# Expert weights with neighbouring rows in one partition, in a two-layer diffusion backbone on one core

## The chip, the cores and the metric

The kernel runs on 1 core of one Trainium2 chip, in float32. The metric is the device time of one execution in microseconds (us), as the median of several runs.

## The reference, cut to what matters

Two layers work on 256 latent tokens of width 1024 (and on 256 context tokens in the first layer's mixer). A layer has a mixer (latent attention with an RG-LRU in layer 0, a Hyena convolution in layer 1) and then a mixture of 16 experts, of which each token takes 2. Both halves are modulated by vectors `sh`, `sc`, `g` that come from a conditioning vector `c` and the big matrix `ada_w`.

```
mod = silu(c) @ ada_w[layer] + ada_b[layer]          # 6 vectors of 1024: sh1, sc1, g1, sh2, sc2, g2
x = x + g1 * mixer(rms_norm(x, norm1_g) * (1 + sc1) + sh1)
h = rms_norm(x, norm2_g) * (1 + sc2) + sh2
s = sigmoid(h @ router_w) ...                        # 16 scores, best group of 4, best 2 in it
for e in range(16):
    y = y + gates[..., e:e+1] * ((silu(h @ w1[e]) * (h @ w3[e])) @ w2[e])
x = x + g2 * y
```

`w1[e]` and `w3[e]` are 1024 x 512, `w2[e]` is 512 x 1024: 2 MiB each, 6 MiB an expert, 192 MiB (201 million bytes) for both layers. Every expert's weights are loaded in full.

## The kernel before, in words

The width of 1024 is contracted 128 rows at a time, with a row of the weights in each of 128 partitions. Everything that meets a weight is therefore cut into 8 chunks (`k`), and chunk `k` holds features `128k` to `128k + 127`. `mat` gives the DMA's source: for `w1` and `w3` a tile of 1 MiB has four chunks, so a partition receives 4 rows that lie 128 rows apart, each a run of 512 floats (2 KB) in HBM; for `w2` a tile has two chunks, 2 runs of 1024 floats (4 KB). In the last pass `w2` is cut by columns and its runs are of 2 KB.

**Loads.** All big loads are planned in `order` and issued one after the other from SP by `emit` (L219). They go into rings of 1 MiB buffers: `w` (9 buffers), `sp` (8, shared with activations), `x` (`extra`, 1 in layer 0 and 3 in layer 1). A load waits at SP for the matmuls that still read its buffer. Experts 4 to 15 are sorted by load at run time, and their loads take the expert's number from a register.

**A mixture of experts** (`moe`) has 7 passes (`PASSES`), six with two experts and one with four. A pass runs `up` for `w1` (L1244), `silu`, `up` for `w3` (L1244), `times` (L1254), `turn` (four transposes, L1259, that bring the hidden activation's 512 features to partitions), `down` (L1272), `weigh` (L1278 to L1282: gates and `g2`, split into a high and a low half for TensorE) and `back` (L1289, L1291: adds to `x`). Tokens are picked by a one-hot matrix `P` in `gather` (L1204, L1215), which contracts the normalised tokens `yh` and `yl` (high and low halves, made by `high`, L627 on ACT, and `low_`, L633 on DVE) and applies the modulation (L1218, L1220). In layer 0 the passes are interleaved with the building of the Hyena filters (L1443, L1470, L1499, L1500).

**The router** stands ahead of it: `enter` (L576 to L580) transposes `x` in 16 pieces, `weights` (L589) multiplies by the router's weights, `choose` (L655 to L663) ranks, `count` (L670 to L677) counts and gives each token a place, `sort`, `gates` and `rounds` follow. Between `in_order("PAD")` in `run` and the `in_order` that ends it in `moe`, the order of TensorE, ACT and DVE is written out by hand; elsewhere a planner with a simulated clock chooses each engine's order from what is ready.

**The modulation in the background.** `bg` does steps of `ada_step`: a matrix's products are summed over `k` on DVE (L451) or TensorE (L442, then ACT L446). Some steps later the 128 partial sums are added up: by transposes and a reduction (`ada_columns`, L372, L379 to L384) for `sh` and `sc`, or by a matmul with ones (`ada_row`, after a DVE instruction L422 that adds the bias; L391, L392) for `g`. At the start of each mixture one matrix is worked through by `bg(KD)`: `sc2` of layer 1 in layer 0, `g2` of layer 1 in layer 1. `bg_all()` then finishes it.

Of the kernel before, what the change touches and what calls it, by code (L numbers as in the profile page):

```python
# [9 lines left out]
F32 = mybir.dt.float32  # L10
# [4 lines left out]
OP = mybir.AluOpType  # L15
# [11 lines left out]
PASSES = ((0, 1), (2, 3), (8, 9), (4, 5, 6, 7), (10, 11), (12, 13), (14, 15))  # L27
LAST = len(PASSES) - 1
QUAD = 4
NW = 9  # L30
N8 = 8
NX = (1, 3)
# [61 lines left out]
def _pack_params(v):  # L94
    pk = np.zeros((128, NPK), np.float32)

    def cols(name, a):
        a = np.asarray(a)
        pk[:a.shape[0], PK[name]:PK[name] + a.shape[1]] = a

    def chunks(a):
        return np.asarray(a).reshape(-1, 128).T

    cols("c", chunks(v["c"]))
    cols("cc", chunks(v["c_ctx"]))
    cols("n1", chunks(v["norm1_g"]))
    cols("n2", chunks(v["norm2_g"]))
    cols("qn", chunks(v["mla_q_norm_g"]))
    cols("kvn", chunks(v["mla_kv_norm_g"]))
    cols("cw", chunks(v["lru_conv_w"]))  # L110
    cols("cb", chunks(v["lru_conv_b"]))
    cols("ba", chunks(v["lru_b_a"]))
    cols("bx", chunks(v["lru_b_x"]))
    cols("lam", chunks(v["lru_lambda"]))
    cols("hw", chunks(v["hy_conv_w"]))
    cols("hb", chunks(v["hy_conv_b"]))
    cols("rb", np.broadcast_to(np.asarray(v["router_b"])[None, :], (128, 16)))
    cols("rw", np.asarray(v["router_w"]).reshape(8, 128, 16).transpose(1, 0, 2).reshape(128, 128))
    cols("adab", chunks(v["ada_b"]))
    cols("dec", chunks(v["hy_decay"]))  # L120
    cols("skip", chunks(v["hy_skip"]))
    cols("b1", np.asarray(v["hy_b1"]).reshape(64, 1))
    cols("f1", np.asarray(v["hy_freq1"]).reshape(64, 1))
    cols("b2", np.tile(np.asarray(v["hy_b2"]).reshape(64, 1), (2, 1)))
    cols("f2", np.tile(np.asarray(v["hy_freq2"]).reshape(64, 1), (2, 1)))
    cols("w1", np.asarray(v["hy_w1"])[0])
    cols("w2", np.asarray(v["hy_w2"])[0])
    return pk
# [38 lines left out]
def build(tc, A, dbg=None, stop=None):  # L167
# [43 lines left out]
    def emit(n):  # L211
        for _ in range(n):
            if emitted[0] < len(order):
                key, src, shape = order[emitted[0]]
                emitted[0] += 1
                i = emitted[0] - 1
                t = apart[i]() if i in apart else wp.tile([128, 2048], F32, tag="w", name=nm("w"))
                v = t[:shape[0], :shape[1] * shape[2]].rearrange("p (k f) -> p k f", k=shape[1])
                nc.sync.dma_start(v, src() if callable(src) else src)  # L219
                made[key] = v  # L220

    def get(key):
# [47 lines left out]
            if len(order) < end:  # L270
                plan(key, src, shape)

    def expert(nme, l, e, r0, nk, c0, nf):

        w = A["moe_" + nme]
        if e < STATIC:
            return mat(w[l, e], r0, nk, c0, nf)
        return lambda: mat(w[l, bass.ds(chosen[l][e - STATIC], 1)].rearrange("o k f -> (o k) f"), r0, nk, c0, nf)

    def moe_tiles(l):  # L280
        for j, es_ in enumerate(PASSES):
            for nme in ("w1", "w3"):
                for kk in range(2):
                    for e in es_:
                        yield ((nme, l, e, kk), expert(nme, l, e, kk * 512, 4, 0, 512), (128, 4, 512))
            for h in range(2):
                for e in es_:
                    if j < LAST:
                        yield (("w2", l, e, h), expert("w2", l, e, h * 256, 2, 0, 1024), (128, 2, 1024))
                    elif h == 0:  # L290
                        yield (("w2", l, e, 0), expert("w2", l, e, 0, 4, 0, 512), (128, 4, 512))
            if j == LAST:
                for h in range(2):
                    for e in es_:
                        yield (("w2", l, e, 1 + h), expert("w2", l, e, h * 256, 2, 512, 512), (128, 2, 512))

    plan_moe(0)
    for n in range(6):
# [69 lines left out]
    def ada_columns(l, s, hf, use, e, four, n):  # L368

        p2 = ps()  # L370
        for m in range(4):
            T.transpose(p2[:, m * 128:m * 128 + 128], e[:, m * 128:m * 128 + 128], ident)  # L372
        pv = p2.rearrange("p (m q r) -> p m q r", m=4, q=4)
        b = pc("adab", l * 48 + s * 8 + hf * 4, 4)
        for i in range(n):
            kind = ("c" if i else "") + ("1" if s < 3 else "2")
            o = mc(l, use + kind)[:, hf * 4:hf * 4 + 4]
            if four:
                V.tensor_reduce(o, pv[:, :, :, i], axis=mybir.AxisListType.X, op=OP.add)  # L379
            else:  # L380
                V.tensor_reduce(o, p2.rearrange("p (m r) -> p m r", m=4), axis=mybir.AxisListType.X, op=OP.add)
            V.tensor_tensor(o, o, b, op=OP.add)
            if use == "sc":
                V.scalar_tensor_tensor(o, o, 1.0, pc("n1" if s < 3 else "n2", l * 8 + hf * 4, 4),  # L384
                                       op0=OP.add, op1=OP.mult)
# [82 lines left out]
    def bg_all():  # L468
        while ada_step():
            pass  # L470
# [68 lines left out]
    def in_order(engines=""):  # L539
# [3 lines left out]
        if engines:  # L543
            manual.append(tc.manual_schedule(engines={ENG[e] for e in engines}))
            manual[0].__enter__()

    class router:


# [21 lines left out]
        def enter(self, i):  # L571

            t, n = divmod(i, 2)
            p = ps()
            for k in range(4):
                T.transpose(p[:, k * 128:k * 128 + 128], x[:, t, (4 * n + k) * 128:(4 * n + k) * 128 + 128], ident)  # L576
            S.activation(self.alloc().bitcast(BF16)[:, :512], x[:, t, n * 512:n * 512 + 512], AF.Square,
                         accum_out=self.ss[:, i:i + 1])
            self.xT[i] = self.alloc()
            S.activation(self.xT[i], p, AF.Copy)  # L580
# [42 lines left out]
        def high(self, t):  # L623

            for n in range(2):
                c = slice(n * 512, n * 512 + 512)
                S.activation(self.y[0][:, t, c], x[:, t, c], AF.Copy, scale=self.r[t])  # L627

        def low_(self, t):

            for n in range(2):
                c = slice(n * 512, n * 512 + 512)
                V.scalar_tensor_tensor(self.y[1][:, t, c], x[:, t, c], self.r[t], self.y[0][:, t, c].bitcast(F32),  # L633
                                       op0=OP.mult, op1=OP.subtract)

        def rank(self, v, n, out):

# [523 lines left out]
    def moe(l, route, ws, filler=None, fills=((0, 0, 0),) * 8, budget=0, late=None, prepare=None, finish=None):  # L1161
# [94 lines left out]
        def turn(j):  # L1256
            p = ps()
            for k in range(4):
                T.transpose(p[:, k * 128:k * 128 + 128], act[j][:, k * 128:k * 128 + 128], ident)  # L1259
            at = act[j] = w2("at")  # L1260
            for i in range(2):
                copy(i, at[:, 256 * i:256 * i + 256], p[:, 256 * i:256 * i + 256])
# [50 lines left out]

        def again(nme, e, k, n=0):
            t = wk.tile([128, 512], F32, tag="t2", name=nm("wr"), bufs=WT2[l])
            nc.sync.dma_start(t, A["moe_" + nme][l, e, k * 128:k * 128 + 128, n * 512:n * 512 + 512])
            return t

        ada_alloc[0] = lambda n, *shape: [w2(n) for _ in range(2)]
# [5 lines left out]
        gather(0, firsts, True)  # L1325
        in_order(ORDER[1 + 2 * l])
        next(steps, None)
        bg_all()
        route.gates()
        route.sort(w2("srt"))  # L1330
        _, chosen[l] = nc.values_load_multi_w_load_instructions(
# [6 lines left out]
        for j in range(LAST + 1):  # L1338
            up(j, "w1", first, firsts)
            a = silu(j)  # L1340
            if j == LAST:
                with tc.issue_after(a.ins):
                    S.activation(warm, ones[:, 0:1], AF.Sqrt)
            if j:
                back(j - 1, 0)
                back(j - 1, 1)
            else:
                slots(0, gate, firsts)
                slots(1, gate, firsts)
            fill(fills[j][0])  # L1350
            up(j, "w3", first, firsts)
            times(j)
            if j % 2 and j < LAST:
                d = j // 2 + 1
                place(d, pos, firsts)
                gather(d, firsts)
                for i in range(2 * d, min(2 * d + 2, LAST + 1)):
                    slots(i, gate_, firsts)
                fill(fills[j][1] - 1)
            else:  # L1360
                fill(fills[j][1])
            turn(j)
            fill(fills[j][2])
            down(j, 0, first, firsts)
            weigh(j, 0)
            if j == LAST:
                fill(99)
                down(j, 1, first, firsts, (0, 1))
                back(j, 0, (0,))
                back(j, 1, (0,))  # L1370
                if late:
                    late(0)
                squares(0)
                down(j, 1, first, firsts, (2, 3))
            else:
                down(j, 1, first, firsts)
            weigh(j, 1)
# [395 lines left out]
```

## Time and profile before

| | us |
|---|---|
| median of 3 runs | 947.39 (945.4 to 949.32) |
| the profiled execution's own time | 945.29 |
| its span, first to last instruction | 943.4 |
| TensorE (PE) busy | 863.5 (92%) |
| DVE busy | 462.8 (49%) |
| ACT busy | 228.9 (24%) |

The granted TensorE clock was 0.975 of full speed over the span. All DMA moved 289.33 MB in 130567 packets, 307 GB/s over the span. A matmul's end is modelled, so PE's busy time also covers starts that are further apart than they need to be. The layers' mixtures run from about 260 to 520 us and from about 697 to 932 us.

### The profile page before, as it was taken

The page shows a single profiled execution, that of the slowest core. Times are in us where ns is not written, and L with a number is a line of the kernel's source. Part 1 is how long each engine was busy: PE and PEld are TensorE (multiplying, and loading weights), DVE is VectorE, ACT ScalarE, POOL GpSimd, SP SyncE. Part 2 cuts the span into 40 slices and gives each one's busy share as a digit, 9 for nine tenths or more (in the row PEclk, how much of TensorE's full clock was granted, in tenths as well). Part 3 has the DMA queues.
Part 4 walks back from the last instruction along what each step waited for, and adds up shares of the span by engine and source line. Part 5 has one row for each costly group of instructions (what it writes and reads, how often), then busy time and mean ns, then how long its engine had stood idle before and what let it go on. Part 6 is the DMA issues. An engine that isn't in the chain of part 4 may idle for free. (4 is left out here: it accounts for less than half of the span.)

```text
span 943.4 us, 10841 instructions
## 1 busy us (share of the span) xinstructions
PE 863.5 (92%) x3976; PEld 447.2 (47%) x3976; DVE 462.8 (49%) x1124; ACT 228.9 (24%) x446; POOL 15.7 (2%) x21
## 2 busy tenths in 40 slices
PE   3998999999999999899998599999989999988984
PEld 2345655574553534333433487776553532423431
DVE  5469785771643454536433648756272323122123
ACT  3276414430411221313122222211031110100112
POOL 0000000000000010101000000000000000000000
PEclk9999999999899999999999799999979999999998
DMA  9957689476799999999999673643199999999993
GB/s 351 353 187 248 224 269 369 165 248 242 244 385 397 329 384 387 395 390 396 396 338 372 229 267 131 223 151 116 57 386 352 389 395 387 404 389 396 396 387 144
DMA packets 130567, 289.33 MB, mean 307 GB/s; under 512 B 6828, under 2 KB 8876, under 8 KB 130500
## 3 DMA queue, kind: packets, MB, share of 16 engines
q1 hardware_dynamic: 129428, 286.39, 82.9%
q10 hardware_dynamic: 1072, 2.10, 0.7%
q8 instruction: 36, 0.59, 0.3%
q14 instruction: 31, 0.25, 0.1%
HBM read 287.42 MB, written 1.05 MB: 306 GB/s over the span
## 5 line engine op out<-in xcount | busy, mean ns | idle before, releaser
L1244 PE MATMUL ps<-w,xe 128*64 128x512 f32 (+1 forms) x696 | 174.6, 597 | 2.4 <-DMA w<-in_moe_w 2.4
L1244 PEld LDWEIGHTS ps<-w,xe 128*64 128x64 f32 (+1 forms) x696 | 50.4, 129 | 87.5 <-issue 79.2
L1272 PE MATMUL ps<-w,at 128*64 128x512 f32 (+1 forms) x344 | 86.0, 597 | 4.5 <-DMA w<-in_moe_w 2.7
L1594 PE MATMUL ps<-xt,w 128*128 128x256 f32 x384 | 87.4, 388 | 1.8 <-ACT xt L1558 1.8
L1594 PEld LDWEIGHTS ps<-xt,w 128*128 128x128 f32 x384 | 74.4, 195 | 14.6 <-ACT xt L1558 2.1
L1291 DVE TENSOR_TENSOR x<-x,ps 128x512 f32<-128x512 f32 x56 | 36.9, 683 | 64.6 <-PE ps L1289 64.6
L1278 DVE SCALAR_TENSOR_TENSOR ye<-ps,gs,grow 128x512 f32<-128x512 f32 x28 | 20.9, 748 | 83.1 <-PE ps L1272 83.1
L1244 PE MATMUL ps<-sp,xe 128*64 128x512 f32 (+1 forms) x216 | 54.5, 598 | 1.4 <-DMA sp<-in_moe_w 1.2
L451 DVE SCALAR_TENSOR_TENSOR e<-w,sg,e 128x512 f32<-128x512 f32 x70 | 51.4, 744 | 3.0 <-DMA w<-in_ada_w 2.3
L1272 PEld LDWEIGHTS ps<-w,at 128*64 128x64 f32 (+1 forms) x344 | 26.7, 130 | 50.6 <-issue 40.0
L1280 ACT ACTIVATE yeh<-ye 128x512 fp32r<-128x512 f32 x28 | 17.6, 630 | 117.5 <-DVE ye L1278 117.5
L1244 PE MATMUL ps<-x,xe 128*64 128x512 f32 (+1 forms) x112 | 37.4, 595 | 1.6 <-DMA x<-in_moe_w 1.6
L1254 DVE TENSOR_TENSOR th<-th,ps 128x512 f32<-128x512 f32 x14 | 9.6, 687 | 59.0 <-PE ps L1244 59.0
L1244 PEld LDWEIGHTS ps<-sp,xe 128*64 128x64 f32 (+1 forms) x216 | 16.7, 132 | 30.0 <-issue 26.3
L1220 ACT ACTIVATE xe<-ps,modc 128x256 f32<-128x256 f32 (+1 forms) x32 | 15.8, 539 | 58.0 <-DVE xe L1218 58.0
L517 PE MATMUL ps<-w,x 128*128 128x512 f32 x64 | 28.4, 595 | 0.7 <-ACT x L1608 0.7
L1249 ACT ACTIVATE th<-ps 128x512 f32<-128x512 f32 x14 | 8.4, 597 | 84.1 <-PE ps L1244 68.5
L835 PE MATMUL ps<-hT,w 128*128 128x512 f32 x64 | 28.0, 593 | 0.4 <-DMA w<-in_ev_w_in 0.4
L517 PE MATMUL ps<-w,mix 128*128 128x512 f32 x64 | 28.2, 594 | 0.0
L1272 PE MATMUL ps<-sp,at 128*64 128x512 f32 (+1 forms) x112 | 26.0, 598 | 2.3 <-ACT at L345 1.7
L442 PE MATMUL ps<-w,cs 128*32 128x512 f32 x160 | 27.1, 714 | 0.0
L930 PE MATMUL ps<-w,hT 128*128 128x288 f32 (+1 forms) x96 | 26.8, 434 | 0.0
(355 smaller groups left out, 1311.0 us busy)
## 6 DMA issues: line engine op xcount, KB each, us to landing
w<-in_moe_w SPq DMA_DIRECT2D x126, 1024.0 KB, 13.9
w<-in_ada_w SPq DMA_DIRECT2D x48, 1024.0 KB, 7.3
sp<-in_moe_w SPq DMA_DIRECT2D x41, 1024.0 KB, 14.6
x<-in_moe_w SPq DMA_DIRECT2D x21, 1024.0 KB, 14.2
w<-in_od_w_in SPq DMA_DIRECT2D x12, 1024.0 KB, 6.8
w<-in_ev_w_in SPq DMA_DIRECT2D x4, 1024.0 KB, 10.9
w<-in_ev_w_out SPq DMA_DIRECT2D x4, 1024.0 KB, 7.9
w<-in_moe_w SPq DMA_DIRECT2D x8, 512.0 KB, 9.8
```

Of the source, the lines that this page charges most:

```text
L442: T.matmul(part[hf][32 * q:32 * q + 32, :], cs[:, k - 3 + q, :], get(("ada", l, s, hf, k // 4))[:, q, :], start=(k == 3), stop=(k == 7), t ...
L451: V.scalar_tensor_tensor(eh, w[hf], c, eh, op0=OP.mult, op1=OP.add)
L517: T.matmul(po[t][n], a[:, k, t * 128:t * 128 + 128], b[:, n * 512:n * 512 + 512], start=(k == korder[0] and i == 0), stop=(k == korder[-1] ...
L835: T.matmul(uxp[b], get(("wux", hf))[:, k % 4, b * 128:b * 128 + 128], hT[hf][:, k % 4, :], start=(k == 0), stop=(k == KD - 1))
L930: T.matmul(p[:, :n], hT[k // 4][:, k % 4, t * 128:t * 128 + 128], get((w, k // 4))[:, k % 4, :], start=(k == 0), stop=(k == KD - 1))
L1220: S.activation(e[:, k, :w], p[:, w:2 * w], AF.Identity, scale=sc[:, k:k + 1], bias=sh[:, k:k + 1])
L1244: T.matmul(p[room * i:room * i + room, :], xe[j // 2][:, k, o:o + room], weight(nme, e, k), start=(k == 0), stop=(k == KD - 1), tile_posit ...
L1272: T.matmul(p[room * i:room * i + room, :], act[j][:, o:o + room], weight("w2", e, k, n), start=(k == 0), stop=(k == 3), tile_position=(0, ...
L1278: V.scalar_tensor_tensor(e, po[j, n], gs[j], grow[l, 5][:, n * 512:n * 512 + 512], op0=OP.mult, op1=OP.mult)
L1280: S.activation(h, e, AF.Copy)
L1291: V.tensor_tensor(xs, xs, p, op=OP.add)
L1594: T.matmul(pb, w[:, k % 4, b * 128:b * 128 + 128], hT[:, k, :], start=(k == 0 and b % 2 == 0), stop=(k == KD - 1 and b % 2 == 1))
```

## The change

The contraction is cut otherwise: a partition now holds neighbouring rows. For `w1` and `w3` partition `p` of tile `a` gets rows `512a + 4p` to `512a + 4p + 3`, and for `w2` rows `256h + 2p` and `256h + 2p + 1`, which is 8 KB in one stretch of HBM and 8 KB in one stretch of the partition. Only the last pass's `w2`, cut by columns, keeps runs of 2 KB; its one tile with two blocks is issued as two DMAs. Chunk `k` then holds every fourth feature of a 512 (every second of a 256 for `w2`), and all that meets it is reordered to match: the router's transposes read `x` with a step of 4 floats, `high` and `low_` read `x` with a step of 4 and write in the new order, `turn` reads with a step of 2, the transposes of `ada_columns` read with a step of 4 for the modulation of the mixture (`s >= 3`), and `norm2_g`, `ada_b` and `router_w` are packed in the new order on the host. Apart from that, `bg_all()` stands later in `moe`: after `up` for `w1`, `silu` and `slots` of the first pass, instead of ahead of `gates` and `sort`. The kernel before already sums some matrices' modulation on TensorE; this is not part of the change.

```diff
+GROUP = {"w1": 4, "w3": 4, "w2": 2}
...
+    def by_rows(a):
+        return np.asarray(a).reshape(-1, 128, 4).transpose(1, 0, 2).reshape(128, -1)
...
-    cols("n2", chunks(v["norm2_g"]))
+    cols("n2", by_rows(v["norm2_g"]))
...
-                nc.sync.dma_start(v, src() if callable(src) else src)
+                a = src() if callable(src) else src
+                if len(a.shape) == 3:
+                    nc.sync.dma_start(v, a)
+                else:
+                    g = a.shape[2]
+                    for b in range(a.shape[1]):
+                        nc.sync.dma_start(v[:, b * g:b * g + g], a[:, b])
...
+    def expert_rows(w, nme, c0, nf):
+        return w.rearrange("(a p k) f -> p a k f", p=128, k=GROUP[nme])[:, :, :, c0:c0 + nf]
...
-            return mat(w[l, e], r0, nk, c0, nf)
+            return expert_rows(w[l, e], nme, c0, nf)[:, a0:a0 + na]
...
-            T.transpose(p2[:, m * 128:m * 128 + 128], e[:, m * 128:m * 128 + 128], ident)
+            T.transpose(p2[:, m * 128:m * 128 + 128], e[:, m * 128:m * 128 + 128] if s < 3 else e[:, m::4], ident)
...
+    def by_rows(v):
+        return v.rearrange("p (k q) -> p k q", k=4)
...
-                T.transpose(p[:, k * 128:k * 128 + 128], x[:, t, (4 * n + k) * 128:(4 * n + k) * 128 + 128], ident)
+                T.transpose(p[:, k * 128:k * 128 + 128], x[:, t, n * 512 + k:n * 512 + 512:4], ident)
...
-                S.activation(self.y[0][:, t, c], x[:, t, c], AF.Copy, scale=self.r[t])
+                S.activation(by_rows(self.y[0][:, t, c]), x[:, t, c].rearrange("p (q k) -> p k q", k=4), AF.Copy,
+                             scale=self.r[t])
...
-                V.scalar_tensor_tensor(self.y[1][:, t, c], x[:, t, c], self.r[t], self.y[0][:, t, c].bitcast(F32),
-                                       op0=OP.mult, op1=OP.subtract)
+                V.scalar_tensor_tensor(by_rows(self.y[1][:, t, c]), x[:, t, c].rearrange("p (q k) -> p k q", k=4),
+                                       self.r[t], by_rows(self.y[0][:, t, c].bitcast(F32)), op0=OP.mult, op1=OP.subtract)
...
-                T.transpose(p[:, k * 128:k * 128 + 128], act[j][:, k * 128:k * 128 + 128], ident)
+                T.transpose(p[:, k * 128:k * 128 + 128], act[j][:, k // 2 * 256 + k % 2:k // 2 * 256 + 256:2], ident)
...
         next(steps, None)
-        bg_all()
         route.gates()
...
                 slots(0, gate, firsts)
                 slots(1, gate, firsts)
+                bg_all()
```

## Rows read from the trace of the kernel before

**Rows 1.** The page, parts 2 and 5: DMA in 40 slices; the costliest matmuls (mean ns).

```profile
GB/s 351 353 187 248 224 269 369 165 248 242 244 385 397 329 384 387 395 390 396 396 338 372 229 267 131 223 151 116 57 386 352 389 395 387 404 389 396 396 387 144
...
L1244 PE MATMUL ps<-w,xe 128*64 128x512 f32 (+1 forms) x696 | 174.6, 597 | 2.4 <-DMA w<-in_moe_w 2.4
```

**Rows 2.** Windows, second mixture; the last columns are granted clock, DMA share, GB/s.

```profile
720.00:925.00 205.00, 188.40 (x914) 73.65 (x912) 52.67 (x99) 22.47 (x44) 0.00 (x0) 1.00 1.04 394
```

**Rows 3.** PE's waits on loads from 265 to 932 us: total, times, longest.

```profile
PE ps L1272 <- DMA w<-in_moe_w: 2.7, 4, 0.7
...
PE ps L1244 <- DMA w<-in_moe_w: 2.4, 2, 1.5
...
PE ps L1244 <- DMA x<-in_moe_w: 1.6, 1, 1.6
...
PE ps L1244 <- DMA sp<-in_moe_w: 1.2, 1, 1.2
...
PE ps L1272 <- DMA sp<-in_moe_w: 0.6, 1, 0.6
```

**Rows 4.** Timeline of PE: first and last of the first mixture's three such waits.

```profile
386.47 0.63 PE L1244 MATMUL ps<-w,xe 128*32 128x512 f32 x3 [1.51 <-DMA w<-in_moe_w]
...
406.96 3.62 PE L1272 MATMUL ps<-w,at 128*32 128x512 f32 x20 [0.68 <-DMA w<-in_moe_w]
```

**Rows 5.** Timeline of PE at the last such wait: start, duration of the group.

```profile
910.48 3.26 PE L1244 MATMUL ps<-sp,xe 128*64 128x512 f32 x13
914.99 3.22 PE L1244 MATMUL ps<-sp,xe 128*64 128x512 f32 x13 [1.25 <-DMA sp<-in_moe_w]
```

**Rows 6.** DMA from 785 to 790 us, while runs of 2 KB land.

```profile
DMA packets 976, 1.94 MB, mean 387 GB/s; under 512 B 31, under 2 KB 31, under 8 KB 976
```

**Rows 7.** DMA from 810 to 815 us, while runs of 4 KB land.

```profile
DMA packets 531, 2.05 MB, mean 410 GB/s; under 512 B 31, under 2 KB 31, under 8 KB 531
```

**Rows 8.** Timeline of SP's queue: the issue of one load of 1 MiB.

```profile
690.69 0.37 SPq L219 DMA_DIRECT2D w<-in_moe_w  x1
```

**Rows 9.** DMA in the first 20 us: ACT's queue (packets, MB) and its one load.

```profile
q10 hardware_dynamic: 144, 0.52, 6.7%
...
fixed<-in_dft ACTq DMA_DIRECT2D x1, 512.0 KB, 5.6
```

**Rows 10.** The page, part 3: a queue that loads instructions: packets, MB, share.

```profile
q8 instruction: 36, 0.59, 0.3%
```

**Rows 11.** Lines L1619 (transposes with a step of 2) and L1259: min/median/max ns.

```profile
L1619 PEld LDWEIGHTS ps<-kc,u x32: 194/207/210, 556.1 to 612.9; 128*128 128x128 f32 x32
...
L1259 PEld LDWEIGHTS ps<-kc,th x56: 137/140/223, 281.3 to 919.7; 128*128 128x128 f32 x56
```

**Rows 12.** The chain that ended last: 8 transposes of L1619, 4 of L576.

```profile
574.62 0.94 PE ps L1619 x8
...
682.59 0.44 PE ps L576 x4
```

**Rows 13.** Lines L627, L633, L1684 (steps of 2) and L1291: ns.

```profile
L627 ACT ACTIVATE yh<-x,rs x8: 706/707/722, 247.9 to 690.0; 128x512 fp32r<-128x512 f32 x8
...
L633 DVE SCALAR_TENSOR_TENSOR yl<-x,rs,yh x8: 743/745/747, 253.7 to 700.2; 128x512 fp32r<-128x512 f32 x8
...
L1684 DVE TENSOR_TENSOR x<-x,ps x4: 674/683/689, 647.9 to 664.5; 128x512 f32<-128x512 f32 x4
...
L1291 DVE TENSOR_TENSOR x<-x,ps x56: 672/680/689, 297.2 to 933.1; 128x512 f32<-128x512 f32 x56
```

**Rows 14.** Timeline of DVE in the second router.

```profile
693.76 0.74 DVE L422 SCALAR_TENSOR_TENSOR e<-fixed,kc,e 24x512 f32<-24x512 f32 x1 [2.10 <-ACT e L446]
694.42 0.17 DVE L660 TENSOR_REDUCE sm<-rg 128x8 f32<-128x32 f32 x1
```

**Rows 15.** Windows around it, columns as in rows 2.

```profile
693.00:697.00 4.00, 1.15 (x11) 0.33 (x4) 3.07 (x11) 1.19 (x2) 0.00 (x0) 1.00 1.02 389
...
700.00:704.00 4.00, 4.00 (x12) 2.45 (x12) 4.00 (x23) 0.60 (x1) 0.00 (x0) 0.50 1.03 415
```

More of the change, by code (lines that the diff above doesn't have):

```diff
@@ L117, in _pack_params @@
     cols("rb", np.broadcast_to(np.asarray(v["router_b"])[None, :], (128, 16)))
-    cols("rw", np.asarray(v["router_w"]).reshape(8, 128, 16).transpose(1, 0, 2).reshape(128, 128))
-    cols("adab", chunks(v["ada_b"]))
+    cols("rw", np.asarray(v["router_w"]).reshape(2, 128, 4, 16).transpose(1, 0, 2, 3).reshape(128, 128))
+    ab = np.asarray(v["ada_b"]).reshape(2, 6, 1024)
+    cols("adab", np.concatenate([(chunks if s < 3 else by_rows)(ab[l, s]) for l in range(2) for s in range(6)], axis=1))
     cols("dec", chunks(v["hy_decay"]))
@@ L271, in plan_moe, with expert @@
                 plan(key, src, shape)
-    def expert(nme, l, e, r0, nk, c0, nf):
+    def expert_rows(w, nme, c0, nf):
+        return w.rearrange("(a p k) f -> p a k f", p=128, k=GROUP[nme])[:, :, :, c0:c0 + nf]
+    def expert(nme, l, e, a0, na, c0, nf):
         w = A["moe_" + nme]
         if e < STATIC:
-            return mat(w[l, e], r0, nk, c0, nf)
-        return lambda: mat(w[l, bass.ds(chosen[l][e - STATIC], 1)].rearrange("o k f -> (o k) f"), r0, nk, c0, nf)
+            return expert_rows(w[l, e], nme, c0, nf)[:, a0:a0 + na]
+        return lambda: expert_rows(w[l, bass.ds(chosen[l][e - STATIC], 1)].rearrange("o k f -> (o k) f"), nme, c0, nf)[:, a0:a0 + na]
     def moe_tiles(l):
@@ L284, in moe_tiles @@
                     for e in es_:
-                        yield ((nme, l, e, kk), expert(nme, l, e, kk * 512, 4, 0, 512), (128, 4, 512))
+                        yield ((nme, l, e, kk), expert(nme, l, e, kk, 1, 0, 512), (128, 4, 512))
             for h in range(2):
@@ L288, in moe_tiles @@
                     if j < LAST:
-                        yield (("w2", l, e, h), expert("w2", l, e, h * 256, 2, 0, 1024), (128, 2, 1024))
+                        yield (("w2", l, e, h), expert("w2", l, e, h, 1, 0, 1024), (128, 2, 1024))
                     elif h == 0:
-                        yield (("w2", l, e, 0), expert("w2", l, e, 0, 4, 0, 512), (128, 4, 512))
+                        yield (("w2", l, e, 0), expert("w2", l, e, 0, 2, 0, 512), (128, 4, 512))
             if j == LAST:
@@ L294, in moe_tiles @@
                     for e in es_:
-                        yield (("w2", l, e, 1 + h), expert("w2", l, e, h * 256, 2, 512, 512), (128, 2, 512))
+                        yield (("w2", l, e, 1 + h), expert("w2", l, e, h, 1, 512, 512), (128, 2, 512))
     plan_moe(0)
@@ L1315, in again @@
             t = wk.tile([128, 512], F32, tag="t2", name=nm("wr"), bufs=WT2[l])
-            nc.sync.dma_start(t, A["moe_" + nme][l, e, k * 128:k * 128 + 128, n * 512:n * 512 + 512])
+            g = GROUP[nme]
+            nc.sync.dma_start(t, expert_rows(A["moe_" + nme][l, e], nme, n * 512, 512)[:, k // g, k % g])
             return t
```

## Prediction

> **What bounds the kernel now.** I read the page first. In its slices the DMA rate is near 390 GB/s in two long plateaus, the two mixtures, and far lower around them [rows 1]. PE is busy for 92% of the span. Both look full, so the question is which of them waits for the other. From 720 to 925 us the DMA share is 1.04, that is, the queues never run dry, and 394 GB/s is all they give there [rows 2]. The view of waits then says what this costs PE: over both mixtures 9 waits on expert weights, 2.7 + 2.4 + 1.6 + 1.2 + 0.6 = 8.5 us [rows 3]. Three of them lie in the first mixture, from one of 1.51 at 386.47 us to one of 0.68 at 406.96, with one of that size between them [rows 4]: 2.9 us, so that 5.6 us in 6 waits are left for the second. A wait shown is shorter than the time lost. At 910.48 us 13 matmuls take 3.26 us; each lasts about 0.6 us by itself [rows 1], so the other 12 starts are (3.26 - 0.6) / 12 = 0.22 us apart, the next start was due at 910.48 + 13 x 0.22 = 913.34, and it came at 914.99: 1.65 us late, where the row says 1.25 [rows 5]. I add 0.38 us to each of the 9 waits, 3.4 us, and get 8.5 + 3.4 = 11.9 us that PE starves. So the mixtures are nearly balanced: PE does work almost throughout, and DMA is late by a little. This is the first thing to see: a faster DMA can bring back 11.9 us, and no more, because behind it stands PE's own work.
>
> **The loads.** What does a longer run do to the rate? The kernel has both lengths in the same saturated queue. While runs of 2 KB land, 5 us bring 976 packets at 387 GB/s [rows 6]; while runs of 4 KB land, 531 packets at 410 GB/s [rows 7]. Over 16 engines that is 16 x 2048 B / 387 GB/s = 84.7 ns for one packet of 2 KB and 159.8 ns for one of 4 KB, so 75.1 ns for each 2 KB and 9.6 ns for each packet. A packet of 8 KB would take 4 x 75.1 + 9.6 = 310 ns, and the rate would be 423 GB/s. No load of the program has such a packet, so I bound it: from below, a packet stays at 4 KB, 410 GB/s; from above 423. A stretch like that from 720 to 925 us at 394 GB/s then shrinks by 205 x (1 - 394/410) = 8.0 us or by 205 x (1 - 394/423) = 14.1 us at its end. In the second mixture PE lacks 5.6 + 6 x 0.38 = 7.9 us: even the lower bound pays that, barely. In the first one PE lacks 4 us after DMA has long been saturated; either bound pays it. I take 423, because packet times grow so evenly from 2 to 4 KB. The last pass's `w2` keeps its 2 KB, and one tile in each layer becomes two DMAs, two more in each layer on SP's queue. An issue takes 0.37 us [rows 8], and the queue stands waiting for PE's buffers there; without that cover the four would cost 1.5 us. I take 10 of the 11.9 us, as part of a starved stretch will turn into waits for ACT and DVE that the starving now covers.
>
> Does the hardware see one run of 8 KB when the pattern is written as four rows? In the first 20 us, ACT's queue loads a 512 KB tile written as 8 pieces of 128 floats in each partition, that lie side by side on both ends; the queue shows 144 packets [rows 9]. Pieces of 512 B would be 1024. It is 128 packets of 4 KB and one small one for each of 16 engines, so neighbouring pieces are merged.
>
> **A rule against it.** The row above has 410 GB/s for one core [rows 7]. The Trainium skill ("DMA: Bandwidth & Descriptors", Specifications) gives about 358 GB/s as what HBM leaves a core. By that rule the loads would be at their limit and the change would bring nothing from here; the trace is already above it.
>
> **The reordered reads.** Transposes: 56 in `turn` (14 passes x 4) get a step of 2; 32 in `enter` (2 layers x 16) and 32 in `ada_columns` (4 matrices x 8) get a step of 4. The trace has transposes with a step of 2: their weight load takes 207 ns, against 140 [rows 11], but loads overlap matmuls, and in the chain 8 of them take 0.94 us, 117 ns each, where 4 with a step of 1 take 0.44, 110 ns each [rows 12]. So 120 x 7.5 ns = 0.9 us, on PE, which is full. Step 4 is in no row; the upper bound is that the whole difference of 67 ns comes through each time: 8.0 us. I take 0.9, since the chain shows the cover.
>
> `high` and `low_`: 8 instructions each of 707 and 745 ns [rows 13]. On a layer's path to `gather` stand two of each (the first token half's); the other two run beside matmuls. DVE with a step of 2 shows no cost: 683 ns in L1684 against 680 in L1291, which has none [rows 13]. Lower bound 0; upper bound a doubling, 2 layers x (2 x 0.707 + 2 x 0.745) = 5.8 us. I take a fifth, 1.2 us, as the nearest row says none but has half the step.
>
> At a step of 2 DVE loses nothing and PE's weight load a half of its time again [rows 11, 13]. The Trainium skill ("Advanced Engine Details and Errata", Memory Cachelines) says that SBUF is read in lines of 16 bytes, at full rate only with two hits on a line. By this rule a step of 2 floats is free, which PE's row contradicts, and a step of 4 is not, so that only `turn` would be spared: by it my sum goes to its upper bound for `high` and `low_`, 4.6 us more. No row here has a step of 4.
>
> **`bg_all()` moved.** Its work is the same: in layer 0 eight transposes with small DVE work, in layer 1 two L422, four L391 and two ACT copies. In the second router DVE stands 2.10 us for the ACT result that L422 reads, works 0.74 us, and only then does L660, the next step of choosing experts [rows 14]; PE has 1.15 us of work in 4 us there, and the granted clock is at half from 700 to 704 us [rows 15]. If L422 goes behind, L660 comes 2.10 + 0.74 = 2.84 us earlier, and what is late next is PE's L670, then `gather`. If the clock then did not fall, the 4 us at half speed give up to 2 more. But L422 is behind L660 in the program already, and the planner put it ahead as a thing that seemed ready; a later place in the program need not change that. Lower bound 0 (PE must do L391 at some time, and in a full stretch it costs the same there), upper bound 4.8. I take 1.0. The new wait it could add is `weigh` of the first pass on the row of `g2`; a whole pass stands between.
>
> **Sum.** Against the profiled execution (945.29 us, span 943.4): -10.0 + 0.9 + 1.2 - 1.0 = -8.9, so 936.4. The median of the runs is 947.39, 2.1 above it; so the forecast is 947.39 - 8.9 = 938.5. Half a per cent, 4.7 us, is about what a measurement of this kernel can tell from no change.
>
> **The rivals.**
> A. The DMA gain does not arrive: packets stay at 2 KB because patterns with a register are not merged, or the rate ends where it is. For it: no packet of a load is over 4 KB; against: the rates and the merged load [rows 7, 9]. Then only the costs are left: +0.9 + 1.2 - 1.0 = +1.1, 948.5; at the upper bounds of both, 0.9 to 8.0 and 1.2 to 5.8, 960. 12%. The Trainium skill's limit for HBM, above, would be a case of A.
> B. The steps of 4 take the gain back: between -8.9 and its upper bounds, -10 + 8.0 + 5.8 - 1.0 = +2.8. For it: PE's 207 ns [rows 11]; against: L1684 [rows 13]. Half-way, -3.0, 944.4. 13%. The Trainium skill's rule on lines, above, speaks for B.
> C. The planner, whose order follows its simulated loads, shifts the passes so that PE waits for `turn` or `yeh` elsewhere. New waits of the size of the second mixture's on loads, 7.9 us, leave -8.9 + 7.9 = -1.0, 946.4. 10%.
> D. Longer packets are slower, not faster: this ends on the other side. The queue of 36 packets of 16 KB has 0.3% of 16 x 943.4 us, 45 us, 1.26 us a packet: 16 engines at 13 GB/s, 208 in all [rows 10]. They carry instructions and not weights, which speaks against it. The point from which it decides is the 394 GB/s of now; at 370, the second mixture's stretch would be 205 x (394/370 - 1) = 13.3 us longer and the first one's about as much, 972. 4%.
> E. `bg_all()` brings its upper bound and PE all 11.9: -11.9 + 2.1 - 4.8 = -14.6, 932.8. 7%.
> The forecast, 934 to 943, holds the rest, 54%.
>
> **How the numbers follow.** The range takes in the forecast's own 934 to 943, E down to 931, and B, C and the middle of A up to 949; D and the end of A are left out. Faster by over 0.5% (below 942.7): the forecast, E and a third of B, 65%. Within 0.5%: the rest of B, C and most of A, 25%. Slower: D and the ends of A and C, 10%.
>
> **What would show it.** Right: DMA in the mixtures at about 420 GB/s with packets of 8 KB; packets in all down by 49152 (for `w1`, `w3`) + 7168 (for `w2`), to some 74,250; no PE waits on expert weights; a DMA share that falls under 1 as the queue waits for PE; the second mixture some 7 to 8 us shorter and the first 3 to 4. Steps of 4: weight loads near 207 ns in L372 and `enter`, `low_` near 745. `bg_all()`: L660 ahead of L422. Wrong: 387 GB/s still; `low_` or `high` well over 1 us; PE waits that name ACT or DVE in place of loads.

## The result, and the profile after

The changed kernel takes 932.35 us, median of 4 runs (932.04 to 932.79), beside 947.06 for the kernel before on the same chip (4 runs, 945.4 to 949.32): a ratio of 0.9844, 95% interval 0.9823 to 0.9865. That is 14.7 us less; the forecast was 8.9 less. The profiled execution has a span of 930.4 us instead of 943.4.

The page first, parts 1 to 3: PE's busy time, DMA in 40 slices, packets.

```profile
PE 850.6 (91%) x3976; PEld 446.0 (48%) x3976; DVE 466.2 (50%) x1124; ACT 232.5 (25%) x446; POOL 15.7 (2%) x21
...
GB/s 354 357 191 249 232 226 367 152 295 249 208 392 408 302 366 398 400 421 420 418 290 340 317 288 120 248 160 90 91 274 353 424 421 421 421 421 421 420 407 109
DMA packets 74312, 289.34 MB, mean 311 GB/s; under 512 B 6892, under 2 KB 8940, under 8 KB 50692
```

Windows of the second mixture, with the columns of [rows 2] (start and end, length, busy us and number of instructions of PE, PEld, DVE, ACT and POOL, granted clock, DMA share, GB/s):

```profile
720.00:820.00 100.00, 95.46 (x524) 40.21 (x521) 29.01 (x59) 12.49 (x25) 0.00 (x0) 1.00 1.01 422
820.00:880.00 60.00, 54.95 (x262) 22.76 (x258) 15.87 (x28) 6.23 (x13) 0.00 (x0) 1.00 1.01 421
```

DMA from 785 to 790 us, which answers to [rows 6]:

```profile
DMA packets 288, 2.10 MB, mean 419 GB/s; under 512 B 32, under 2 KB 32, under 8 KB 32
```

The plateaus of [rows 1] went from 390 to 421 GB/s, and 74312 - 50692 = 23620 packets now have 8 KB or more: the rows are merged, behind a register's address too. PE's waits on loads from 265 to 932 us, in [rows 3] 9 of them and 8.5 us, are down to 3 and 1.7:

```profile
PE ps L1292 <- DMA w<-in_moe_w: 1.1, 2, 0.6
...
PE ps L1264 <- DMA x<-in_moe_w: 0.6, 1, 0.6
```

To see where the 13.0 us of the span come from, I cut both executions at fixed matmuls: the first transpose of `enter`, the first `up`, and the four transposes of `turn`, one group in each of a mixture's seven passes. Starts are from the timeline of PE, in us.

| from | to | before | after | difference |
|---|---|---|---|---|
| start | `enter`, layer 0 | 242.66 | 244.15 | +1.5 |
| `enter` | first `up` | 22.40 | 22.09 | -0.3 |
| first `up` | first `turn` | 16.27 | 17.74 | +1.5 |
| first `turn` | seventh | 225.57 | 222.96 | -2.6 |
| seventh `turn` | `enter`, layer 1 | 175.53 | 174.45 | -1.1 |
| `enter` | first `up` | 25.63 | 23.49 | -2.1 |
| first `up` | first `turn` | 16.26 | 18.41 | +2.2 |
| first `turn` | seventh | 195.10 | 182.62 | -12.5 |
| seventh `turn` | end | 24.02 | 24.49 | +0.5 |

So nearly all of it lies between the first and the seventh `turn` of the second mixture. Its fourth to seventh group, before and then after:

```profile
816.14 0.66 PE L1259 MATMUL ps<-kc,th 128*128 128x128 f32 x4 [0.81 <-DVE th L1254]
...
855.63 0.66 PE L1259 MATMUL ps<-kc,th 128*128 128x128 f32 x4 [0.78 <-DVE th L1254]
...
889.08 0.65 PE L1259 MATMUL ps<-kc,th 128*128 128x128 f32 x4 [0.78 <-DVE th L1254]
...
919.42 0.66 PE L1259 MATMUL ps<-kc,th 128*128 128x128 f32 x4 [0.78 <-DVE th L1254]
```

```profile
815.26 0.74 PE L1279 MATMUL ps<-kc,th 128*128 128x128 f32 x4 [0.82 <-DVE th L1274]
...
844.82 0.74 PE L1279 MATMUL ps<-kc,th 128*128 128x128 f32 x4 [0.78 <-DVE th L1274]
...
877.89 0.74 PE L1279 MATMUL ps<-kc,th 128*128 128x128 f32 x4 [0.78 <-DVE th L1274]
...
905.91 0.75 PE L1279 MATMUL ps<-kc,th 128*128 128x128 f32 x4 [0.79 <-DVE th L1274]
```

From the fourth to the fifth 39.49 us became 29.56, from the sixth to the seventh 30.34 became 28.02. The first of these holds the `down` of the pass with four experts. The timeline of PE shows it, before and after (start, duration of the group, operation; matmuls of four experts use four different strips of the array, each of 128 rows and 32 columns, which is the 128*32 of the row):

```profile
817.52 6.30 PE L1272 MATMUL ps<-sp,at 128*32 128x512 f32 x36 [0.73 <-ACT at L345]
824.41 1.90 PE L1272 MATMUL ps<-sp,at 128*32 128x512 f32 x4 [0.58 <-DMA sp<-in_moe_w]
826.97 1.90 PE L1272 MATMUL ps<-w,at 128*32 128x512 f32 x4 [0.65 <-DMA w<-in_moe_w]
829.53 0.62 PE L1272 MATMUL ps<-w,at 128*32 128x512 f32 x1 [0.66 <-DMA w<-in_moe_w]
...
830.89 2.27 PE L1272 MATMUL ps<-w,at 128*32 128x512 f32 x5
833.08 1.07 PE L1244 MATMUL ps<-w,xe 128*64 128x512 f32 x2
```

```profile
816.64 4.08 PE L1292 MATMUL ps<-sp,at 128*32 128x512 f32 x34 [0.64 <-ACT at L361]
820.13 0.99 PE L1292 MATMUL ps<-w,at 128*32 128x512 f32 x2
...
823.15 0.98 PE L1292 MATMUL ps<-w,at 128*32 128x512 f32 x2
824.06 1.07 PE L1264 MATMUL ps<-w,xe 128*64 128x512 f32 x2
```

The same 64 matmuls (4 experts x 4 chunks x 2 halves are 32 in the program; each leaves two in the trace), in the same written order, take 15.6 us before (817.52 to 833.08) and 7.4 after. After, the first 34 take 4.08 us: four experts side by side. Before, the tiles arrive one by one about 2.56 us apart (824.41, 826.97, 829.53), and on each arrival four matmuls of one expert run alone, 1.90 us for 4. The waits shown are 0.58 + 0.65 + 0.66 = 1.9 us; the loss is 8.1. The rest of it stands in the trace as PE's own work. The windows of this one line from 817.4 to 825 us, before and after (length, PE, PEld, granted clock, DMA share, GB/s), say it in two numbers:

```profile
817.40:825.00 7.60, 6.89 (x38) 1.80 (x39) 1.00 1.02 408
```

```profile
817.40:825.00 7.60, 6.73 (x60) 2.17 (x53) 1.00 1.02 423
```

PE is as busy in both, with 38 matmuls in the one and 60 in the other.

### The profile page after: what moved, and what is told of

Its sections match the earlier page's. It is cut to its first block, busy times and chain, and to the rows that moved or that the text cites. A ratio compares the mean times of both kernels' runs of the same rounds, so it can differ in the third digit from the quotient of the medians.

```text
span 930.4 us, 10857 instructions
## 1 busy us (share of the span) xinstructions
PE 850.6 (91%) x3976; PEld 446.0 (48%) x3976; DVE 466.2 (50%) x1124; ACT 232.5 (25%) x446; POOL 15.7 (2%) x21
## 2 busy tenths in 40 slices
DMA packets 74312, 289.34 MB, mean 311 GB/s; under 512 B 6892, under 2 KB 8940, under 8 KB 50692
## 5 line engine op out<-in xcount | busy, mean ns | idle before, releaser
L1302 DVE TENSOR_TENSOR yel<-ye,yeh 128x512 fp32r<-128x512 f32 x28 | 19.3, 691 | 15.7 <-ACT yeh L1300 10.5
L1309 PE MATMUL ps<-yeh,st 128*128 128x512 f32 x56 | 21.8, 435 | 4.7 <-ACT yeh L1300 4.7
## 6 DMA issues: line engine op xcount, KB each, us to landing
sp<-in_moe_w SPq DMA_DIRECT2D x39, 1024.0 KB, 15.6
```

Of the source, the lines that this page charges most:

```text
L1302: V.tensor_tensor(o, e, h.bitcast(F32), op=OP.subtract)
L1309: T.matmul(p, st[j][:, t * 128:t * 128 + 128], ye[j, n][i], start=(i == 0), stop=(i == 1))
```

## The experiments

Theory: late loads cost far more than the waits show, since experts whose tiles come late run one at a time; so each per cent of the loads' rate counts while PE is late. First rival, the prediction's own: PE lacks 11.9 us, and any rate from 410 GB/s on pays that. Second rival: the order of work or the moved `bg_all()` brought the gain. Below, "fourth to fifth" and the like are starts of `turn` as above.

**Run length alone.** Two kernels keep all of the changed one (its order of matmuls but for one) and load other rows into the tiles:

```diff
-            return expert_rows(w[l, e], nme, c0, nf)[:, a0:a0 + na]
+            return mat(w[l, e], a0 * g * 128, na * g, c0, nf)                             # 2 KB (w2: 4 KB)
+            return w[a0 * 512:a0 * 512 + 512].rearrange("(b p k) f -> p b (k f)", b=2, k=2)  # 4 KB
```

Runs of 2 KB:

> The changed kernel with everything as it is, its order of matmuls too, but the experts' weights loaded as before the change (rows of one partition 128 apart: runs of 2 KB for w1 and w3, 4 KB for w2). So weight rows and activations no longer belong together and the result is not the mixture; the work is the same. Theory (the loads' rate is the whole gain): DMA back at 390 to 395 GB/s from 720 to 900 us, the downs of the pass with four experts spread over about 15 us again where the changed kernel has 7, and a time of 946 to 950. Rival (the order of work or the moved transposes brought the gain): it stays within 3 of the changed kernel, 932 to 936.

947.36 us, 1.004 of the kernel before (1.0011 to 1.0069), as the theory has it. Runs of 4 KB:

> As the run with 2 KB runs, but w1 and w3 come in runs of 4 KB (two neighbouring rows in a partition, twice for each tile) and w2 in runs of 4 KB, one DMA for each tile still; the result again is not the mixture. The rate should be near 410 GB/s. Theory (PE follows the loads from 816 us to the end, so that every per cent of rate counts): the stretch of 205 us ends 205 x (1 - 394/410) = 8.0 us earlier than before the change instead of 205 x (1 - 394/421) = 13.1, so the time is about 5 above the changed kernel, 936 to 939. Rival (the prediction's: PE lacks 11.9 us and either bound pays it): within 1.5 of the changed kernel, 931 to 934.

938.92 us, ratio 0.9931 (0.9906 to 0.9956), again in the theory's range. Their windows from 720 to 820 us (2 KB, then 4 KB), with the columns of [rows 2]:

```profile
720.00:820.00 100.00, 95.46 (x522) 40.58 (x519) 28.99 (x59) 12.51 (x25) 0.00 (x0) 1.00 1.04 395
```

```profile
720.00:820.00 100.00, 95.47 (x514) 40.08 (x513) 29.00 (x59) 12.10 (x25) 0.00 (x0) 1.00 1.03 409
```

The second rival falls with the first of them: layout, order and `bg_all()` without the rate bring nothing. The first falls with the second: at 409 GB/s the time is 6.5 us below the kernel before, less than half of the 14.7. A part of that gap lies outside the mixtures; from first to seventh `turn` alone the two mixtures are 2.0 + 7.8 = 9.8 us shorter than before, where the changed kernel has 2.6 + 12.5 = 15.1. Where the rate counts is seen in the three intervals in which the two kernels differ most:

| interval | before | 2 KB | 4 KB | 8 KB |
|---|---|---|---|---|
| first mixture, third to fourth | 50.40 | 50.54 | 48.35 | 47.16 |
| second mixture, fourth to fifth | 39.49 | 38.41 | 33.77 | 29.56 |
| second mixture, sixth to seventh | 30.34 | 30.50 | 28.29 | 28.02 |

The last is nearly paid by 409 GB/s already, the two others are not: in them lie the `up` of the four-expert pass (first mixture) and its `down` (second mixture). In the 4 KB run tiles still come one by one in that `down`; two of its rows (timeline of PE, as above):

```profile
819.09 5.37 PE L1304 MATMUL ps<-sp,at 128*32 128x512 f32 x40 [0.63 <-ACT at L373]
824.01 1.90 PE L1304 MATMUL ps<-w,at 128*32 128x512 f32 x4
```

**`bg_all()` alone**, on the old layout:

```diff
         next(steps, None)
-        bg_all()
         route.gates()
...
                 slots(1, gate, firsts)
+                bg_all()
```

> The kernel before with one edit, bg_all() moved into the first pass. Theory (what leaves the second gather comes back in the first pass: 2.1 us shorter up to the first up, 2.2 longer by the next pass): 946 to 948, no change. Rival (the prediction's upper bound for this edit, 4.8 us): 942 to 943.

945.16 us, ratio 0.9998 (0.9974 to 1.0021): no change, as the theory has it (the kernel before took 945.44 on that chip). From the first `up` to the first `turn` it takes 17.57 and 18.42 us instead of 16.27 and 16.26: the 1.3 and 2.2 us that the change shows there are this work, in its new place. What it leaves behind in the routers can't be read from single profiles: from `enter` to the first `up` of the second layer the kernel before has 25.63 us and this one 26.36, and other runs with either place of `bg_all()` lie between 22.3 and 25.0. The granted clock is another in each: 0.80 over that stretch in the kernel before, 0.68 in this run, 0.85 in the changed kernel. So the 2.1 us that the change shows there may in part be the clock.

**The order of `high` and `low_`.** First in natural order:

```diff
-                S.activation(by_rows(self.y[0][:, t, c]), x[:, t, c].rearrange("p (q k) -> p k q", k=4), AF.Copy, scale=self.r[t])
+                S.activation(self.y[0][:, t, c], x[:, t, c], AF.Copy, scale=self.r[t])
...
+                V.scalar_tensor_tensor(self.y[1][:, t, c], x[:, t, c], self.r[t], self.y[0][:, t, c].bitcast(F32), ...)
```

> The changed kernel with high and low_ writing the token rows in their natural order, reads and writes with a step of 1, so the gathered features no longer match the weights and the result is not the mixture. Theory (two of each stand on the path to each gather: 2 x (1.2 - 0.7) + 2 x (1.145 - 0.745) = 1.8 us a layer): both gathers start 1 to 2 us earlier against the end of enter, and the time is 2 to 4 below the changed kernel, 928 to 930.5. Rival (the loads set the end of the second mixture, and what is won ahead of it is only waited for there): the first layer's 1 to 2 us, 930.5 to 932.5.

931.68 us (930.04 to 934.55), ratio 0.9869 (0.9833 to 0.9905): in the rival's range, but not to be told from the changed kernel's 0.9844. So both were run again side by side:

> The changed kernel once more, beside the next run on the same chip. Expected of both theories: ratio 0.984 within 0.003.

> Once more the changed kernel with high and low_ in natural order (its result is not the mixture), beside the changed kernel on the same chip, since the first run of it could not be told from the changed kernel. Theory (the loads set the end of the second mixture from 715 us on, so that only what comes earlier in the first layer is kept): 0 to 2 below the changed kernel. Rival (both layers' 1.8 us are on the path): 3.0 to 4.0 below.

933.47 us, ratio 0.9868 (0.984 to 0.9896), for the changed kernel, and 930.91, 0.9851 (0.9821 to 0.988), for the natural order. The change itself is worth 13.1 us on this chip (946.60 for the kernel before). The natural order is 2.6 us below the changed kernel, between the two ranges that were expected, and the intervals overlap, so the times do not give the price of the reordered reads. The profiles give it for the first layer. From `enter` to the first `up` there, the changed kernel takes 22.09 and 22.14 us in its two profiles and the natural order 20.01 and 20.03; here the first of each:

```profile
244.15:266.24 22.09, 16.86 (x125) 13.37 (x123) 17.99 (x86) 11.71 (x22) 0.00 (x0) 0.92 1.00 363
```

```profile
242.71:262.72 20.01, 16.87 (x126) 13.38 (x124) 16.50 (x86) 9.76 (x22) 0.00 (x0) 0.91 0.98 363
```

PE is busy for the same time at nearly the same clock, while DVE and ACT have 1.5 and 2.0 us less: 2.1 us for this layer. In the second layer the same stretch takes 23.49 us twice in the changed kernel, at a clock of 0.85, and 23.81 and 24.99 in natural order, at 0.78 and 0.73, so no price can be read there. The instructions themselves are clear: in the changed kernel, answering to [rows 13],

```profile
L646 ACT ACTIVATE yh<-x,rs x8: 1208/1255/1268, 249.6 to 690.3; 128x512 fp32r<-128x512 f32 x8
...
L653 DVE SCALAR_TENSOR_TENSOR yl<-x,rs,yh x8: 1117/1145/1171, 255.7 to 699.7; 128x512 fp32r<-128x512 f32 x8
```

With two rows in a stretch, all steps are 2 and `w1` and `w3` come in 4 KB:

```diff
-GROUP = {"w1": 4, "w3": 4, "w2": 2}
+GROUP = {"w1": 2, "w3": 2, "w2": 1}
...
-                T.transpose(..., x[:, t, n * 512 + k:n * 512 + 512:4], ident)
+                T.transpose(..., x[:, t, n * 512 + k % 2 * 256 + k // 2:n * 512 + k % 2 * 256 + 256:2], ident)
```

> The change with two rows in a stretch instead of four: w1 and w3 in runs of 4 KB, w2 in its runs of 4 KB as before, one DMA for each tile, and all reordered reads with a step of 2; the result is the reference's. Beside the run with 4 KB runs and steps of 4 it prices the steps. Theory (DVE and ACT pay for a step of 4 and not for one of 2): low_ 745 to 800 ns and high 700 to 800, the weight loads in enter still near 207, and 936 to 939, 0 to 2 below the run with steps of 4. Rival (a step of 2 costs as much): low_ over 1.0 us and no difference.

935.26 us, ratio 0.9893 (0.9857 to 0.9929), a little below the expected 936 to 939 and 3.7 below the run with 4 KB and steps of 4, more than expected, though the two intervals overlap. The interval also overlaps both of the changed kernel's (0.9823 to 0.9865 and 0.984 to 0.9896), so what 8 KB with steps of 4 brings over 4 KB with steps of 2 is not settled by the times. The rival is out: the run's two rows are nearly those of [rows 13]:

```profile
L645 ACT ACTIVATE yh<-x,rs x8: 737/756/781, 250.2 to 690.2; 128x512 fp32r<-128x512 f32 x8
...
L652 DVE SCALAR_TENSOR_TENSOR yl<-x,rs,yh x8: 741/744/747, 256.3 to 698.7; 128x512 fp32r<-128x512 f32 x8
```

Then with the step moved from the reads of `x` to the writes:

```diff
-                S.activation(by_rows(self.y[0][:, t, c]), x[:, t, c].rearrange("p (q k) -> p k q", k=4), ...)
+                S.activation(self.y[0][:, t, c].rearrange("p (k q) -> p q k", k=4), x[:, t, c].rearrange("p (q k) -> p q k", k=4), ...)
```

> The changed kernel with high and low_ going through x in its natural order, and writing (low_ reading yh too) with a step of 128 elements; the result is the reference's. Theory (the cost sits in reading one element from each 16 bytes): high back to about 0.7 us; low_, which now reads yh with a long step, still 1.1 or more; time within 1.5 of the changed kernel, 931 to 933.5. Rival (writing apart costs as much as reading apart): high 1.2 or more.

935.35 us, ratio 0.9896 (0.9862 to 0.993), above the expected 931 to 933.5. My theory failed here: a write with a step of 128 costs ACT nearly as much as a read with a step of 4 (`low_` has 1117 ns, as expected).

```profile
L646 ACT ACTIVATE yh<-x,rs x8: 1149/1185/1222, 248.8 to 691.2; 128x512 fp32r<-128x512 f32 x8
```

**Less to load in one pass.** In layer 1's four-expert pass, `w1` and `w3` load half of each tile and use each row twice:

```diff
+    def half(nme, l, e):
+        return l == 1 and nme != "w2" and e in PASSES[3]
...
+                        nk = 2 if half(nme, l, e) else 4
```

> The kernel before, with its runs of 2 KB, but in the second layer the four-expert pass loads only the first half of each tile of w1 and w3 and uses each row twice: 8 MB, or 21 us of DMA at 394 GB/s, less to load, the same matmuls; the result is not the mixture. Theory (late loads cost the second mixture of the kernel before some 12 to 13 us, most of it hidden as PE time, since the four experts' matmuls run side by side only when all four tiles are there): 932 to 935, with the downs of that pass in about 7 us. Rival (the prediction's count from the view of waits, 7.9 us): 937 to 940.

> The changed kernel with the same halved tiles. Theory (at 421 GB/s PE is hardly late any more; what is left is PE's own work): 0 to 2 below the changed kernel, 930 to 932.5, and within 2 of the kernel before with halved tiles. Rival (PE still follows the loads in the changed kernel, so that each faster load still pays): 924 to 928.

On the kernel before: 930.91 us, ratio 0.9841 (0.9803 to 0.9878), 1.1 below the theory's range and far from the rival's, with runs of 2 KB throughout. On the changed kernel: 928.05 us (925.2 to 931.2), ratio 0.983 (0.9797 to 0.9862), at the upper end of the rival's range and 2.9 below the halved kernel before, where the theory had at most 2. But the two kernels also differ from their parents in the order of the matmuls, which the planner makes for the loads that it expects, and the intervals help to separate the two effects:

| second mixture | before | 8 KB | before, half | 8 KB, half |
|---|---|---|---|---|
| third to fourth `turn` | 35.07 | 35.15 | 30.80 | 30.89 |
| fourth to fifth | 39.49 | 29.56 | 29.73 | 27.79 |

Fourth to fifth is mainly the loads: 9.8 us come back without touching the run length, as many as the change brings, and 1.8 more in the changed kernel. The written order of the halved runs differs a little in this `down` too, so these two numbers hold a part of the order; the runs of 2, 4 and 8 KB, which share theirs, show the loads alone. Third to fourth, with the `up` of that pass, is not the rate: 35.1 us at 394, 409 and 421 GB/s alike (35.14 and 35.15 in the 2 and 4 KB runs). The two halved runs, whose written order differs there, have 4.3 less. The timeline of PE shows how: in the changed kernel two matmuls of one expert stand alone, 1.04 us, with no wait ahead of them, and 26 take 3.62; in the one with halved tiles 32 take 3.64. That the order and not the halved tiles brought it is argued from this; no run changed the order alone.

```profile
793.71 1.04 PE L1264 MATMUL ps<-w,xe 128*32 128x512 f32 x2
...
795.82 3.62 PE L1264 MATMUL ps<-w,xe 128*32 128x512 f32 x26
```

```profile
797.17 3.64 PE L1268 MATMUL ps<-w,xe 128*32 128x512 f32 x32
```

**Another place for the four-expert pass:**

```diff
-PASSES = ((0, 1), (2, 3), (8, 9), (4, 5, 6, 7), (10, 11), (12, 13), (14, 15))
+PASSES = ((0, 1), (2, 3), (4, 5, 6, 7), (8, 9), (10, 11), (12, 13), (14, 15))    # early
+PASSES = ((0, 1), (2, 3), (8, 9), (10, 11), (4, 5, 6, 7), (12, 13), (14, 15))    # late
```

> The changed kernel with the four-expert pass one place earlier in both layers (third instead of fourth); the result is the reference's. Theory (from 715 us on the DMA never rests, and the last matmuls wait for the last tiles, so the end is set by the bytes over the rate and not by the place of this pass): within 2 of the changed kernel, 930.5 to 934.5; in the second mixture the delay stands some 25 us earlier. Rival (the loss is made in the four-expert pass alone, by how far the loads are ahead when it begins, and each two-expert pass before it uses up 12 x 2.49 - 27 = 3 us of that): 3 below, 928 to 930.

> The changed kernel with the four-expert pass one place later in both layers (fifth instead of fourth); the result is the reference's. Theory (the bytes over the rate set the end): within 2 of the changed kernel, 930.5 to 934.5. Rival (the loss is made in the four-expert pass alone): 3 above, 935 to 938.

946.68 us early (ratio 1.001, 0.9993 to 1.0027) and 936.92 late (0.9903, 0.9872 to 0.9934). The early run misses both expectations; the late one misses the theory's and lies in the rival's 935 to 938. The second mixture by itself stays within the theory's 2 us, 183.83 and 184.01 us from the first to the seventh `turn` against 182.62; the first mixture, into whose passes other work is filled by their number, takes 236.74 and 224.04 against 222.96. So the late run's time is not the rival's 3 us in the second mixture: of the 5.1 us between the two spans (935.5 and 930.4) 1.4 lie there, 1.1 in the first mixture, and the rest outside these stretches. In the early run the granted clock is 0.96 over that stretch of the first mixture, against 1.00 in the other two, which can be a part of its 13.8 us. I had not thought of that, and did not trace it further.

## Why the prediction was right, and where its size was off

**The time.** 932.35 us lies below the forecast's own 934 to 943. It lies in the stated range only because that was drawn down to 931 for rival E, whose reason did not come. The way and the cause (faster loads, PE late) were right. That the number is inside is luck in part, since the term for the loads was too small.

**Rate.** Right: 419 to 422 GB/s, forecast 423; 74312 packets, forecast 74,250. The 288 packets of 785 to 790 us are 256 of 8 KB and 32 small; at 421 GB/s one of 8 KB takes 16 x 8192 B / 421 GB/s = 311 ns, forecast 310. Rival A is out. The Trainium skill's 358 GB/s for a core ("DMA: Bandwidth & Descriptors", Specifications) does not bound this core: the measured 421 decides.

**What the rate is worth: the term that was mis-sized.** I put it at 10.0 of "11.9 us, and no more, because behind it stands PE's own work". From first to seventh `turn` the two mixtures became 2.6 + 12.5 = 15.1 us shorter. The waits I had listed were all real, but the working behind them, waits plus 0.38 us each, took a busy PE for a PE at its full pace. Of the `down` alone 8.1 us were lost with 1.9 of waits shown. That "even the lower bound pays that, barely" fell with it: the 4 KB run pays 9.8 of the 15.1 us. The first reading, that a stretch of 205 us at 394 GB/s ends 14.1 us earlier, was nearer to the 12.5 measured than the 7.9 that I then set as its bound. Two signs that were to show the forecast right did not come: the DMA share stays at 1.01 instead of falling under 1, and 3 waits on expert weights are left.

**First mixture.** Forecast 3 to 4, measured 3.2 in its one interval, and 2.6 over all passes: the wait at 386 us is gone, the two at 404 and 407 are among the three still there.

**Reordered reads.** Forecast +0.9 for the transposes: a step of 4 costs the weight load no more than a step of 2 [rows 11],

```profile
L595 PEld LDWEIGHTS ps<-kc,x x32: 196/210/262, 243.7 to 685.7; 128*128 128x128 f32 x32
```

and the four of a `turn` take 0.74 us instead of 0.66, 14 x 0.08 = 1.1 us for those 56 alone. So the term is a little over its forecast, and far from the 8.0. For `high` and `low_` the guess of a fifth was wrong: they are 78% and 54% longer, 2 x 0.55 + 2 x 0.40 = 1.9 us a layer on the path, 3.8 in all against 1.2 forecast, of the bound of 5.8. In the first layer it arrives at the first `up` (2.1 us, above); whether the second layer's does, and how much of either reaches the end, could not be measured. The rule on lines of 16 bytes in the Trainium skill ("Advanced Engine Details and Errata", Memory Cachelines), which spoke for rival B, agrees with DVE here: 744 ns at a step of 2, 1145 at 4. PE's weight loads do not follow it: 140, 207 and 210 ns at steps of 1, 2 and 4.

**`bg_all()`.** Forecast -1.0, measured nothing: 0.9998 by itself. As feared, the row's sum (L438 now) still stands ahead of the step of choosing (L680 now), so the 2.84 us were not won; only its wait is shorter than in [rows 14]:

```profile
692.07 0.74 DVE L438 SCALAR_TENSOR_TENSOR e<-fixed,kc,e 24x512 f32<-24x512 f32 x1 [0.71 <-ACT e L462]
692.74 0.17 DVE L680 TENSOR_REDUCE sm<-rg 128x8 f32<-128x32 f32 x1
```

**Rivals.** B came in part, with its price below what the loads brought. C did not: PE's waits on `th`, `at` and `yeh` from 265 to 932 us are 8.1 + 4.5 + 4.3 = 16.9 us before and 8.5 + 4.3 + 4.7 = 17.5 after. D is out, and E's 932.8 is close to the measured time, but not for its reason: `bg_all()` gave nothing, and the loads more than 11.9.

**Left open.** 1.5 us before the first `enter` are of the size by which runs differ (244.15 us in one profile of the changed kernel, 240.80 in the other).

## What to carry to other kernels

Where matmuls of several experts share the array in strips, PE's busy time is no measure of its need: compare how many matmuls a stretch of equal busy time holds, or give the pass less to load and see what comes back. Size a faster load by the time that the queue has been full before the last late tile, at every place where PE is late, and not by the waits in the trace: here that gave 14.1 us for the second mixture, against 7.9 from the waits and 12.5 measured; no other kernel was tried. And once the loads are faster, the order of work that was written for the slow ones is the next thing to look at; here up to 4.3 us in one pass seem to hang on it.

## What had not been expected

- A saturated DMA gains from runs over 4 KB: 394 to 395 GB/s with 2 KB, 409 with 4 KB, 421 with 8 KB.
- On ACT a write with a step of 128 elements costs nearly as much as a read with a step of 4: 1185 and 1255 ns for 128 x 512, against 707 without steps and 756 with a step of 2.
- A weight load of PE takes longer at a step of 2, and hardly longer still at a step of 4: 140, 207, 210 ns.
